# Hybrid decoder layer on one core: v's raw buffers in rising order, two more U steps in the selection, longer runs of V and U products, another order at both ends

## The chip, the cores and the metric

The kernel runs on one core of one Trainium2 chip. The metric is the device time of one launch in microseconds (us). TensorE (PE) does the matrix products, ScalarE (ACT), VectorE (DVE) and GpSimd (POOL) the elementwise work, SyncE (SP) issues most DMAs.

## What is computed

One layer over 512 tokens of width 1024: two token mixers on one input projection, an output projection, then a feed-forward layer that picks for every token and each of 8 heads 16 of 16384 single-neuron experts, and a final norm:

```python
n = rmsnorm(h); proj = n @ w_in; h = h + concat(gla(...), ssd(...)) @ w_out
q = (n2 @ w_query);  s = q . sub_keys            # 2 x 128 scores per token and head
top_s, top_i = top_k(s, 16); best_s, best_pos = top_k(sums of both halves, 16)
gate = softmax(best_s)
out[t] = sum_e gelu(n2[t] . u[e]) * gate[t, e] * v[e]    # e: the chosen experts
y = rmsnorm_final(h + out)
```

## The kernel before

Everything is written in the order in which each engine runs it; there is no scheduler. Products run as three float32r products (`mm3`, lines 107 to 110): each operand is split into a high part (ACT copies it to float32r) and a low part (DVE or POOL subtracts it: `split`, line 102), and hi*hi, hi*lo and lo*hi are summed in PSUM.

Three of the four token tiles (384 tokens) are done densely: all 16384 experts are computed, as 128 blocks of 128, and the gate is zero for those not chosen. The fourth tile goes by indirect DMA: POOL gathers the rows of u and v that each token chose, and DVE multiplies them (`gather`, `use`). The dense blocks have two parts. A **U step** of block e is 24 products of 384 columns (`u_part`, 8 parts of three), whose result goes through a gelu into slot e of `ring`, a buffer of 59 slots. A **V step** of block e is 18 products of 512 columns (`vgrp`, 6 groups of three), which multiply the gated slot e into six PSUM banks (3 token tiles by 2 halves).

The stages in their order, and what the change touches in each:

- *Start.* x is normalised and transposed (`nT`); `ahead` (line 158) loads the blocks of `w_in` into `wraw` and splits them. Block 0 is split inside the loop over `dc`, behind the transposes.
- *Mixers and queries.* Input projection, mixers, output projection, then 16 query blocks with U steps between. Not touched.
- *Selection* (after the queries). DVE's `select(t)` turns places into expert numbers with one-hot tiles (`gat`, float16), `spread(t)` transposes numbers and gates on PE, `spread2(t)` copies them out. Between these calls, `u_run(n)` puts n whole U steps into PE's queue; each one's two low splits run on POOL here.
- *Gates.* For 48 units of 8 tokens, DVE makes one-hot tiles A, eq, B (`gprep`), PE multiplies them to the 128x128 gate tables (`gunit`), DVE multiplies slots 0 to n of `ring` by them, ACT copies the rest: what belongs to blocks 59 to 127 goes into `stage` and in six stores (each 64 tokens) to DRAM (`gd`). U steps run between the units, evenly spread up to block 56; their low splits are on DVE here.
- *V and U.* `vs` is the stream of v (128 blocks, 4 raw buffers, split into pairs). For block e: V groups of half 0, V groups of half 1, and between them the 8 U parts of block e+59. `gload` brings the gates of block e+59 from `gd` into the slot that block e leaves. The pool of v's buffers is made where the pool of A, eq, B and `stage` was closed, so they lie in the same memory.
- *End.* The last two V blocks by token tile (`final`), residual, norm and store; token tile 3 (the gathered one) is ready earlier.

SP issues the DMAs strictly in the order written: a DMA that must wait for its buffer or its data holds all behind it. In `Stream.loads` the raw tiles come from one name with `bufs=nraw`. In the built program the four raw tiles of v are handed out at byte 175424, then 187712, 183616, 179520, of each partition; the two `stage` buffers lie at 171328 to 188992 and 188992 to 206656, and the sixth store reads the second.

The lines of the steps: `Stream.loads` 47, `split` 102, `ahead` 158, `u_part` 1050, `u_run` 1063, the calls of the selection 1087 to 1110, `gunit` 1177, `vs.loads` 1234, `gload` 1251, `final` 1257, the V and U loop 1322 to 1378.

Of the kernel before, what the change touches and what calls it, by code (L numbers as in the profile page):

```python
# [7 lines left out]
F32 = mybir.dt.float32  # L8
F32R = mybir.dt.float32r
# [9 lines left out]
D = 1024  # L19
# [16 lines left out]
class Stream:  # L36
# [9 lines left out]

    def loads(s, upto):
        while s.nl <= min(upto, len(s.src) - 1):
            s.raw[s.nl] = s.c.tile([128, 1024], F32, name=s.nm + "r", bufs=s.nraw)
            s.y.load(s.raw[s.nl], s.src[s.nl])  # L50
            s.nl += 1

# [11 lines left out]
class Layer:  # L64
# [22 lines left out]
    def load(self, out, in_):  # L87
        return self.nc.sync.dma_start(out, in_)
# [10 lines left out]
    def stt(self, out, x, s, y, op0, op1, **k):  # L99
        return self.V.scalar_tensor_tensor(out, x, s, y, op0=op0, op1=op1, **k)  # L100
# [31 lines left out]
    def mixers(self):  # L132
# [104 lines left out]
        def scale(t, half, on_act):  # L237
            x, r = xs[t][:, half * 512:half * 512 + 512], vs_[t][:, 2:3]
            if on_act:
                act(x, x, AF.Copy, scale=r)  # L240
            else:
                V.tensor_scalar(x, x, r, None, op0=OP.mult)
# [13 lines left out]
        scale(2, 0, False)  # L256
        power(vs_[3])
        scale(2, 1, False)
        scale(3, 0, True)
        scale(3, 1, False)  # L260
        nTh, nTl = nt(), nt()
# [3 lines left out]
            for dc in range(8):  # L265
                T.transpose(px[dc][:, t * 128:(t + 1) * 128], xs[t][:, dc * 128:(dc + 1) * 128], ident)
        for dc in range(8):
            if dc == 0:
                ahead(0, 3, 0)
            act(nh[dc], px[dc], AF.Copy, scale=wmix[:, dc:dc + 1])  # L270
            stt(nl[dc], px[dc], wmix[:, dc:dc + 1], nh[dc].bitcast(F32), OP.mult, OP.subtract)
            if dc == 4:
                ahead(0, 3, 1)
# [584 lines left out]
    def experts(self):  # L858
# [117 lines left out]
        def select(t):  # L976

            while any(p[0] == t for p in pieces):
                piece()
            ii = kp.tile([128, 2, 8, 16], F32, name="ii", bufs=2)  # L980
            for e in range(2):
                oh = c.tile([128, 8, 16, 16], F16, name="gat", tag="gat", bufs=3)
                tt(oh, bc(CF[0][:, e, t], 2, 16), bc(itj if e else its, 1, 8), OP.is_equal if e else OP.is_ge)
                tt(oh, oh, TIE[t][:, e], OP.mult)
                for n in (8, 4, 2):
                    tt(oh[:, :, 0:n, :], oh[:, :, 0:n, :], oh[:, :, n:2 * n, :], OP.add)
                tt(ii[:, e], oh[:, :, 0, :], oh[:, :, 1, :], OP.add)
            IX[t] = ii
# [24 lines left out]
        def spread(t):  # L1013
            ii, g = IX.pop(t), bs[:, t]
            p = pt()
            T.transpose(p[:, 0:128], flat(ii[:, 0]), ident)
            T.transpose(p[:, 128:256], flat(ii[:, 1]), ident)
            T.transpose(p[:, 256:384], flat(g), ident)
            act(gs[:, 0, t * 128:(t + 1) * 128], p[:, 256:384], AF.Copy, scale=SC)
            SPR[t] = p  # L1020
# [42 lines left out]
        def u_run(n):  # L1063
            for _ in range(n):
                for i in range(8):
                    u_part(i)
# [27 lines left out]
        ties(2)  # L1094
        u_run(1)
        select(1)
        spread(0)
        u_run(1)
        ties(3)
        select(2)  # L1100
        u_run(2)
# [4 lines left out]
        select(3)  # L1106
        u_run(2)
        spread(2)
        u_run(4)
        spread2(2)  # L1110
        idx = c.tile([128, 128], I32, name="idx")
        gt0 = c.tile([128, 128], F32, name="gt0")
# [118 lines left out]
        vp = ctx.enter_context(tc.tile_pool(name="vp", bufs=1, reuse_waits="tile"))  # L1231
        vs = Stream(self, vp, "v", [a["v"][e * 128:(e + 1) * 128, :] for e in range(NE)], 4)
        HT[0] = htile()
        vs.loads(1)
        u_run(1)
        vs.split(1)
        hprep(0)
        u_run(1)
        vs.loads(3)

        g0 = ng[0]
        share = [0]
# [8 lines left out]
        def gload(e):  # L1251
            if e < NE:
                load(ring[:, e % RS, :], gd3[:, e - RS, :])

        gload(RS)

        def final():

            nv = lambda: c.tile([128, 4], F32, name="rs3", bufs=4)
            hf = [slice(0, 512), slice(512, 1024)]  # L1260
            junk = [c.tile([128, D], F32, name="gat", tag="gat", bufs=3), vp.tile([128, D], F32, name="vr", bufs=4)]
            v = [nv() for _ in range(4)]

            def products(t):
                s = slice(t * 128, t * 128 + 128)
                for n in range(2):
                    for e in (NE - 2, NE - 1):
                        self.mm3(pv[t][n], HT[e][0][:, s], HT[e][1][:, s], *vs.parts[2 * e + n], False, e == NE - 1)

            def residual(t, n):  # L1270
                h = hs[t][:, hf[n]]
                stt(h, pv[t][n], 1.0 / SC, h, OP.mult, OP.add)
                square(t, n)

            def square(t, n):
                act(junk[t % 2][:, hf[n]], hs[t][:, hf[n]], AF.Square, accum_out=v[t][:, n:n + 1])

            def weight(t, n, eng):
                eng.tensor_tensor(hs[t][:, hf[n]], hs[t][:, hf[n]], wf[:, hf[n]], op=OP.mult)

            def mean(t):
                V.tensor_scalar(v[t][:, 2:3], v[t][:, 0:1], EPS * D, None, op0=OP.add)
                V.tensor_scalar(v[t][:, 0:1], v[t][:, 1:2], v[t][:, 2:3], 1.0 / D, op0=OP.add, op1=OP.mult)

            def power(t):
                G.tensor_tensor(v[t][:, 3:4], v[t][:, 0:1], self.mhalf, op=OP.pow)

            def scale(t):
                stt(hs[t], hs[t], v[t][:, 3:4], wf, OP.mult, OP.mult)
                load(self.out[t], hs[t])  # L1290

            square(3, 0)
            square(3, 1)
            mean(3)
            power(3)
            for t in range(3):
                products(t)
            residual(0, 0)
            residual(0, 1)
            scale(3)  # L1300
            mean(0)
            power(0)
            residual(1, 0)
            weight(1, 0, G)
            residual(1, 1)
            weight(1, 1, G)
            scale(0)
            mean(1)
            power(1)
            residual(2, 0)  # L1310
            weight(2, 0, G)
            residual(2, 1)
            weight(2, 1, V)
            act(hs[1], hs[1], AF.Copy, scale=v[1][:, 3:4])
            load(self.out[1], hs[1])
            mean(2)
            power(2)
            act(hs[2][:, hf[0]], hs[2][:, hf[0]], AF.Copy, scale=v[2][:, 3:4])
            V.tensor_scalar(hs[2][:, hf[1]], hs[2][:, hf[1]], v[2][:, 3:4], None, op0=OP.mult)
            load(self.out[2], hs[2])  # L1320

        for e in range(NE):
            todo = [gather] * (plan[e + 1] - plan[e])
            pos = [(2 * i + 1) * 7 // max(1, 2 * len(todo)) for i in range(len(todo))]

            def fill(i, todo=todo, pos=pos):
                while pos and pos[0] <= i:
                    pos.pop(0)
                    todo.pop(0)()

            vs.loads(e + 4)
            if e == NE - 2:

                hprep(e + 1)
                vs.split(2 * e + 2)
                vs.pair = us.pair
                vs.split(2 * e + 3)
                final()
                break
            hh, hl = HT.pop(e)  # L1340

            def vgrp(n, t):
                s = slice(t * 128, t * 128 + 128)
                vh, vl = vs.parts[2 * e + n]
                self.mm3(pv[t][n], hh[:, s], hl[:, s], vh, vl, e == 0, e == NE - 1)

            for i in range(3):
                vgrp(0, i)
                if i == 2:
                    vs.parts.pop(2 * e)  # L1350
                    vs.split(2 * e + 2)
                    hprep(e + 1)
                    gload(e + 1 + RS)
                u_part(i)
                fill(i)
            u_part(3)
            for i in range(3):
                vgrp(1, i)
                if i == 2:
                    vs.parts.pop(2 * e + 1)  # L1360
                    vs.split(2 * e + 3)
                u_part(4 + i)
                fill(3 + i)
            u_part(7)
            fill(6)
            if e == NE - 12:
                for t in (0, 1):
                    hs[t] = us.c.tile([128, D], F32, name="ur", bufs=2)
                    load(hs[t], self.hd[t])
            if e == NE - 4:  # L1370
                while ng[0] < 256 or pend:
                    gather()
                vs.loads(NE - 1)
                wf = c.tile([128, D], F32, name="gat", tag="gat", bufs=3)
                load(wf, a["w_norm_final"].to_broadcast([128, D]))
                hs[2] = c.tile([128, D], F32, name="gat", tag="gat", bufs=3)
                load(hs[2], self.hd[2])
                hs[3] = acc[0]
# [90 lines left out]
```

## Time and profile before

| | us |
|---|---|
| median of 3 runs (lowest, highest) | 1508.53 (1506.76, 1512.19) |
| the profiled execution | 1503.02 |
| its span, first to last instruction | 1501.2 |
| PE busy in it | 1456.2 (97%) |
| DVE busy | 1169.4 (78%) |
| ACT busy | 632.7 (42%) |
| POOL busy | 451.7 (30%) |
| mean granted TensorE clock | 0.991 of 2.4 GHz |

The profile is of one execution, 1.8 us longer outside its span. Matmuls are pipelined and their ends are modelled, so the distance between starts tells the pace of PE. In rows of time the columns are start, duration (us), engine, line, operation and tiles; in brackets the idle time of the engine before it, and what ended it. SPq and ACTq are the queues' own rows: the time at which a DMA is issued, not its transfer.

### The profile page before, as it was taken

Reading aid. Unit: us, or ns where it says so; the run is one execution under the profiler, and the core shown is the slowest. Engines: PE = TensorE matmul, PEld = TensorE weight load, DVE = VectorE, ACT = ScalarE, POOL = GpSimd, SP = SyncE. Lnnn points to the kernel's source line nnn. Section 1 sums busy time; section 2 is a strip of 40 time slices with the busy share of each in tenths; the row PEclk is TensorE's granted clock in tenths of the full one; section 3 lists DMA queues with packets and bytes.
Section 4 is the critical chain, followed back from the end, with each engine's and each line's share of the span. In section 5 each row is a group of like instructions: output and inputs, shape, how many; then the busy total and the mean of one; then the engine's idle time right before and its main releaser. Section 6 shows DMA issues by size and latency. Waiting matters only on the chain.

```text
span 1501.2 us, 22402 instructions
## 1 busy us (share of the span) xinstructions
PE 1456.2 (97%) x7904; PEld 1278.0 (85%) x7904; DVE 1169.4 (78%) x2473; ACT 632.7 (42%) x1201; POOL 451.7 (30%) x380
## 2 busy tenths in 40 slices
PE   7999999999898999979999999999999999999997
PEld 5787778888898999878999999999999998888886
DVE  6542663789999999967877778777788888888886
ACT  5435633433654544433333333333333333444444
POOL 2002404444672000002333333333333333333332
PEclk9999999999999999999999999999999999999999
DMA  5231224222334556658888888889899888888894
GB/s 189 84 126 58 71 73 155 96 85 85 105 104 143 159 167 175 180 181 300 322 316 316 323 312 307 317 305 332 304 331 322 314 316 276 292 300 299 297 325 178
DMA packets 148738, 335.56 MB, mean 224 GB/s; under 512 B 64640, under 2 KB 73872, under 8 KB 148496
## 3 DMA queue, kind: packets, MB, share of 16 engines
q1 hardware_dynamic: 58672, 186.32, 36.1%
q0 software_dynamic: 36864, 134.23, 25.1%
q10 hardware_dynamic: 53088, 13.57, 3.9%
q8 instruction: 62, 1.02, 0.3%
q14 instruction: 52, 0.43, 0.1%
HBM read 315.79 MB, written 18.28 MB: 223 GB/s over the span
## 4 chain that ended last, share of the span: by engine, by line
PE 80%; DVE 12%; issue 3%; DMA 2%; ACT 2%; POOL 0%; SPq 0%; DVEq 0%; POOLq 0%; ACTq 0%
PE pm L109 25%; PE pm L108 25%; PE pm L110 25%; DVE gat L97 4%; PE pg L1186 2%; DVE B L97 1%; DVE ul L104 1%; PE pm L904 1%; DMA gd<-stage 1%; DVE ring L97 1%; DMA ur<-in_uT 1%; DVE eq L97 1%; DVE A L97 1%; ACT b L91 0%; ACT tp L91 0%
## 5 line engine op out<-in xcount | busy, mean ns | idle before, releaser
L108 PE MATMUL pm<-nT,uh 128*128 128x384 f32 (+1 forms) x1152 | 402.1, 349 | 8.8 <-ACT uh L91 8.3
L110 PE MATMUL pm<-nT,ul 128*128 128x384 f32 (+1 forms) x1152 | 397.0, 345 | 2.0 <-POOL ul L104 2.0
L109 PE MATMUL pm<-nT,uh 128*128 128x384 f32 (+1 forms) x1152 | 397.0, 345 | 0.5 <-DVE nT L97 0.5
L109 PE MATMUL pm<-vl,hh 128*128 128x512 f32 x765 | 300.4, 393 | 0.2 <-DVE vl L104 0.2
L110 PE MATMUL pm<-vh,hl 128*128 128x512 f32 x765 | 300.3, 393 | 0.0
L108 PE MATMUL pm<-vh,hh 128*128 128x512 f32 x765 | 299.0, 391 | 0.2 <-ACT vh L91 0.2
L1135 POOL DMA_INDIRECT gat<-in_u,idx x128 | 136.8, 1069 | 473.3 <-DVE gat L100 467.0
L91 ACT ACTIVATE uh<-ur 128x512 fp32r<-128x512 f32 x288 | 180.2, 629 | 214.1 <-PE pm L109 182.0
L108 PEld LDWEIGHTS pm<-nT,uh 128*128 128x128 f32 x1152 | 218.1, 189 | 33.5 <-ACT uh L91 8.7
L109 PEld LDWEIGHTS pm<-nT,uh 128*128 128x128 f32 x1152 | 218.1, 189 | 25.0 <-DVE nT L97 1.1
L110 PEld LDWEIGHTS pm<-nT,ul 128*128 128x128 f32 x1152 | 217.7, 189 | 9.1 <-POOL ul L104 2.9
L1135 POOL DMA_INDIRECT gat<-in_v,idx x128 | 147.2, 1150 | 253.1 <-DVE n2a L100 220.4
L91 ACT ACTIVATE vh<-vr 128x512 fp32r<-128x512 f32 x255 | 159.4, 626 | 136.8 <-PE pm L110 135.4
L104 DVE TENSOR_TENSOR vl<-vr,vh 128x512 fp32r<-128x512 f32 x255 | 175.3, 688 | 37.4 <-ACT vh L91 36.4
L104 DVE TENSOR_TENSOR ul<-ur,uh 128x512 fp32r<-128x512 f32 x206 | 140.7, 689 | 56.8 <-ACT uh L91 56.4
L100 DVE SCALAR_TENSOR_TENSOR n2a<-gat,dots,n2a 128x1024 f32<-128x1024 f32 x128 | 164.0, 1281 | 21.5 <-DMA gat<-in_v,idx 18.5
L110 PEld LDWEIGHTS pm<-vh,hl 128*128 128x128 f32 x765 | 143.7, 188 | 30.9
L100 DVE SCALAR_TENSOR_TENSOR gat<-gat,n2a 128x1024 f32<-128x1024 f32 x128 | 156.2, 1220 | 9.8 <-DMA gat<-in_u,idx 9.6
L108 PEld LDWEIGHTS pm<-vh,hh 128*128 128x128 f32 x765 | 144.0, 188 | 14.2 <-ACT vh L91 0.7
L109 PEld LDWEIGHTS pm<-vl,hh 128*128 128x128 f32 x765 | 144.0, 188 | 14.1 <-DVE vl L104 0.5
L104 POOL TENSOR_TENSOR ul<-ur,uh 128x512 fp32r<-128x512 f32 x82 | 118.7, 1455 | 99.8 <-ACT uh L91 99.4
L91 ACT ACTIVATE gl<-pm 128x384 f32<-128x384 f32 (+16 forms) x104 | 46.0, 442 | 219.8 <-PE pm L110 219.8
(254 smaller groups left out, 1685.2 us busy)
## 6 DMA issues: line engine op xcount, KB each, us to landing
ur<-in_uT SPq DMA_DIRECT2D x128, 512.0 KB, 6.0
vr<-in_v SPq DMA_DIRECT2D x128, 512.0 KB, 5.0
gd<-stage ACTq DMA_DIRECT2D x6, 2208.0 KB, 14.5
ring<-gd SPq DMA_DIRECT2D x69, 192.0 KB, 5.2
wraw<-in_w_in SPq DMA_DIRECT2D x23, 512.0 KB, 4.4
ur<-in_w_query SPq DMA_DIRECT2D x16, 512.0 KB, 3.7
b<-in_x SPq DMA_DIRECT2D x8, 512.0 KB, 3.6
wraw<-in_w_out SPq DMA_DIRECT2D x8, 512.0 KB, 3.9
```

The source lines that it names most:

```text
L91: return self.S.activation(out, in_, f, **k)
L97: return self.V.tensor_tensor(out, x, y, op=op)
L100: return self.V.scalar_tensor_tensor(out, x, s, y, op0=op0, op1=op1, **k)
L104: (self.G if pool else self.V).tensor_tensor(lo, src, hi.bitcast(F32), op=OP.subtract)
L108: T.matmul(out, lhi, rhi, start=start, stop=False)
L109: T.matmul(out, lhi, rlo, start=False, stop=False)
L110: T.matmul(out, llo, rhi, start=False, stop=stop)
L904: T.matmul(p[:, t * 128:(t + 1) * 128], q[:, t * 128:(t + 1) * 128], skT[:, b, :], start=True, stop=True)
L1135: G.indirect_dma_start(out=r, out_offset=None, in_=src, in_offset=bass.IndirectOffsetOnAxis(ap=idx[:, k:k + 1], axis=0))
L1186: T.matmul(o, A[:, t // 2, :, t % 2], B[:, i, t // 2, :, t % 2], start=i == 0, stop=i == 1)
```

## The change

- `Stream.loads`: each raw buffer has its own name, so the tiles lie and are used in rising order (v: 175424, 179520, 183616, 187712).
- Start: block 0 of `w_in` is split in two halves before x's last scaling, ACT then POOL, instead of in the loop behind the transposes.
- Selection: two U steps before `spread(0)` in place of one behind it, and five in place of four before the last `spread2`. Two steps more in all, so the gates stage holds two fewer.
- V: three v blocks are loaded at first in place of two and then two more; the first `gload` moves to the end of block 0's U step, and block 60's with it.
- V and U: three V groups in turn, four U parts, three V groups, four U parts, in place of single groups and parts alternating.
- End: other engines and halves for the last scalings, the last tile stored in two halves, one of them from ACT's queue.

```diff
-            s.raw[s.nl] = s.c.tile([128, 1024], F32, name=s.nm + "r", bufs=s.nraw)
+            s.raw[s.nl] = s.c.tile([128, 1024], F32, name=f"{s.nm}r{s.nl % s.nraw}", bufs=1)
@@ start, before scale(3, ...)
+        parts[0] = b4(F32R), b4(F32R)
+        for k in range(2):
+            f = slice(k * 512, k * 512 + 512)
+            act(parts[0][0][:, f], raws[0][:, f], AF.Copy)
+        for k in range(2):
+            f = slice(k * 512, k * 512 + 512)
+            self.G.tensor_tensor(parts[0][1][:, f], raws[0][:, f], parts[0][0][:, f].bitcast(F32), op=OP.subtract)
+        raws.pop(0)
+        seen[1] = 1
@@
-            if dc == 0:
+            if dc == 1:
                 ahead(0, 3, 0)
@@ selection
         select(1)
+        u_run(2)
         spread(0)
-        u_run(1)
         ties(3)
...
         spread(2)
-        u_run(4)
+        u_run(5)
         spread2(2)
@@ before the V loop
-        vs.loads(1)
+        vs.loads(2)
         u_run(1)
         vs.split(1)
         hprep(0)
         u_run(1)
-        vs.loads(3)
...
-        gload(RS)
-
@@ final
-            weight(1, 1, G)
-            scale(0)
+            residual(2, 0)
+            scale(0, hf[1])
+            load(self.out[0], hs[0])
+            residual(2, 1)
             mean(1)
             power(1)
-            residual(2, 0)
-            weight(2, 0, G)
-            residual(2, 1)
-            weight(2, 1, V)
-            act(hs[1], hs[1], AF.Copy, scale=v[1][:, 3:4])
-            load(self.out[1], hs[1])
+            scale(1, hf[1])
             mean(2)
             power(2)
+            act(hs[1][:, hf[0]], hs[1][:, hf[0]], AF.Copy, scale=v[1][:, 3:4])
+            load(self.out[1], hs[1])
+            weight(2, 0, V)
             act(hs[2][:, hf[0]], hs[2][:, hf[0]], AF.Copy, scale=v[2][:, 3:4])
-            V.tensor_scalar(hs[2][:, hf[1]], hs[2][:, hf[1]], v[2][:, 3:4], None, op0=OP.mult)
-            load(self.out[2], hs[2])
+            self.S.dma_start(self.out[2][:, hf[0]], hs[2][:, hf[0]])
+            scale(2, hf[1])
+            load(self.out[2][:, hf[1]], hs[2][:, hf[1]])
@@ V and U
-            vs.loads(e + 4)
+            vs.loads(e + 4 if e else 2)
...
-                    gload(e + 1 + RS)
+                    if e:
+                        gload(e + 1 + RS)
+                fill(i)
+            for i in range(4):
                 u_part(i)
-                fill(i)
-            u_part(3)
             for i in range(3):
                 vgrp(1, i)
                 if i == 2:
                     vs.parts.pop(2 * e + 1)
                     vs.split(2 * e + 3)
-                u_part(4 + i)
                 fill(3 + i)
+            for i in range(4, 7):
+                u_part(i)
+            if e == 0:
+                gload(RS)
+                gload(RS + 1)
             u_part(7)
```

SP's queue where the V stage begins (`vr` is a raw buffer of v, `ur` one of u, `ring<-gd` a `gload`; the `ur` loads are those of blocks 59 and on). Before:

```order
L88 DMA vr<-in_v 128x1024 x2
L88 DMA ur<-in_uT 128x1024 x2
L88 DMA vr<-in_v 128x1024 x2
L88 DMA ring<-gd 128x384
L88 DMA vr<-in_v 128x1024
```

And now:

```order
L88 DMA vr_6957<-in_v 128x1024
L88 DMA vr_6959<-in_v 128x1024
L88 DMA vr_6961<-in_v 128x1024
L88 DMA ur_6964<-in_uT 128x1024
L88 DMA ur_7010<-in_uT 128x1024
L88 DMA ur_7078<-in_uT 128x1024
L88 DMA ring<-gd 128x384 x2
L88 DMA vr_7133<-in_v 128x1024
```

Three loads of v and three of u now stand ahead of the first `gload`; before it were four of v and two of u, and the second v buffer was the one at byte 187712, half in the second `stage` buffer.

PE's queue in the V and U stage, from the first V group of a block. Before, and the same place now:

```order
L108 MATMUL pm<-vh,hh 128x512
L109 MATMUL pm<-vl,hh 128x512
L110 MATMUL pm<-vh,hl 128x512
L108 MATMUL pm<-nT,uh 128x384
L109 MATMUL pm<-nT,uh 128x384
L110 MATMUL pm<-nT,ul 128x384
```

```order
L108 MATMUL pm<-vh,hh 128x512
L109 MATMUL pm<-vl,hh 128x512
L110 MATMUL pm<-vh,hl 128x512
L108 MATMUL pm<-vh,hh 128x512
L109 MATMUL pm<-vl,hh 128x512
L110 MATMUL pm<-vh,hl 128x512
L108 MATMUL pm<-vh,hh 128x512
L109 MATMUL pm<-vl,hh 128x512
L110 MATMUL pm<-vh,hl 128x512
L108 MATMUL pm<-nT,uh 128x384
```

Nine V products stand in a row, and twelve U products follow; the number of products is the same.

## Rows read from the trace of the kernel before

**Rows 1.** Page, part 1: busy us of each engine

```profile
PE 1456.2 (97%) x7904; PEld 1278.0 (85%) x7904; DVE 1169.4 (78%) x2473; ACT 632.7 (42%) x1201; POOL 451.7 (30%) x380
```

**Rows 2.** Windows: stretch, PE, PEld, DVE, ACT, POOL busy, PEclk, DMA share, GB/s

```profile
380.00:462.00 82.00, 71.95 (x402) 69.90 (x401) 79.66 (x131) 45.26 (x71) 55.51 (x34) 0.98 0.34 116
...
690.00:1440.00 750.00, 750.00 (x3668) 664.39 (x3667) 602.48 (x904) 286.48 (x544) 263.73 (x238) 1.00 0.88 310
```

**Rows 3.** Timeline where the V stage begins, of several engines and queues

```profile
656.49 0.52 ACTq L1199 DMA_DIRECT2D gd<-stage  x1
...
657.78 0.69 DVE L104 TENSOR_TENSOR ul<-ur,uh 128x512 fp32r<-128x512 f32 x1 [0.66 <-ACT uh L91]
...
666.01 0.34 PE L108 MATMUL pm<-nT,uh 128*128 128x384 f32 x1
...
666.53 0.39 PE L108 MATMUL pm<-vh,hh 128*128 128x512 f32 x1
...
669.88 0.33 SPq L88 DMA_DIRECT2D vr<-in_v  x1
...
675.65 0.69 PE L108 MATMUL pm<-nT,uh 128*128 128x384 f32 x1 [8.26 <-ACT uh L91]
...
685.22 0.39 PE L108 MATMUL pm<-vh,hh 128*128 128x512 f32 x1
...
693.54 0.39 PE L108 MATMUL pm<-vh,hh 128*128 128x512 f32 x1
```

**Rows 4.** Page, part 6: DMA issues, count, KB each, median us to landing

```profile
ur<-in_uT SPq DMA_DIRECT2D x128, 512.0 KB, 6.0
...
gd<-stage ACTq DMA_DIRECT2D x6, 2208.0 KB, 14.5
```

**Rows 5.** Waits of PE, 390 to 463 us: total, times, longest

```profile
PE pm L1017 <- DVE ii L97: 3.9, 2, 2.6
PE pg L1186 <- DVE B L97: 3.3, 1, 3.3
...
PE pm L1018 <- DVE bs L97: 1.4, 1, 1.4
```

**Rows 6.** Selection: POOL's splits (397 to 459.7 us, by form), two DVE rows of time

```profile
L104 POOL TENSOR_TENSOR ul<-ur,uh 128x512 fp32r<-128x512 f32 x26 | 44.4, 1722 | 18.7 <-ACT uh L91 18.2 <-PE pm L110 0.2
...
419.48 1.21 DVE L97 TENSOR_TENSOR gat<-tops,itj 128x2048 f16<-128x2048 f16 x1
...
424.68 2.32 DVE L97 TENSOR_TENSOR gat<-tops,its 128x2048 f16<-128x2048 f16 x1
```

**Rows 7.** Gates stage: its window (columns as in Rows 2), and DVE's splits (page, part 5)

```profile
488.00:655.60 167.60, 162.73 (x1354) 153.45 (x1352) 163.67 (x293) 80.99 (x197) 1.15 (x1) 1.00 0.57 164
...
L104 DVE TENSOR_TENSOR ul<-ur,uh 128x512 fp32r<-128x512 f32 x206 | 140.7, 689 | 56.8 <-ACT uh L91 56.4
```

**Rows 8.** The second V product, 690 to 1235 us, then 1245 to 1470 us (by form)

```profile
L109 PE MATMUL pm<-vl,hh 128*128 128x512 f32 x394 | 155.6, 395 | 0.0
...
L109 PE MATMUL pm<-vl,hh 128*128 128x512 f32 x326 | 126.8, 389 | 0.0
```

**Rows 9.** Timeline of the start

```profile
13.67 2.37 POOL L104 TENSOR_TENSOR b<-wraw,b 128x1024 fp32r<-128x1024 f32 x1 [1.78 <-DMA d_skip<-in_d_skip]
...
16.09 0.50 PE L110 MATMUL pm<-nT,b 128*128 128x512 f32 x1 [0.35 <-POOL b L104]
```

**Rows 10.** Timeline of the end

```profile
1492.47 1.28 DVE L100 SCALAR_TENSOR_TENSOR gat<-pm,gat 128x512 f32<-128x512 f32 x2
...
1495.39 0.21 DVE L1283 TENSOR_SCALAR rs<-rs 128x1 f32<-128x1 f32 x1
...
1495.01 1.40 POOL L1279 TENSOR_TENSOR gat<-gat 128x512 f32<-128x512 f32 x1
1496.38 0.54 POOL L1286 TENSOR_TENSOR rs<-rs,mhalf 128x1 f32<-128x1 f32 x1
...
1497.70 0.33 SPq L88 DMA_DIRECT2D out_dram<-gat  x1
```

More of the change, by code (lines that the diff above doesn't have):

```diff
@@ L1260, in final @@
             hf = [slice(0, 512), slice(512, 1024)]
-            junk = [c.tile([128, D], F32, name="gat", tag="gat", bufs=3), vp.tile([128, D], F32, name="vr", bufs=4)]
+            junk = [c.tile([128, D], F32, name="gat", tag="gat", bufs=3), vp.tile([128, D], F32, name=f"vr{NE % 4}", bufs=1)]
             v = [nv() for _ in range(4)]
@@ L1286, in power, with scale @@
                 G.tensor_tensor(v[t][:, 3:4], v[t][:, 0:1], self.mhalf, op=OP.pow)
-            def scale(t):
-                stt(hs[t], hs[t], v[t][:, 3:4], wf, OP.mult, OP.mult)
-                load(self.out[t], hs[t])
+            def scale(t, cols=slice(0, D)):
+                stt(hs[t][:, cols], hs[t][:, cols], v[t][:, 3:4], wf[:, cols], OP.mult, OP.mult)
             square(3, 0)
@@ L1300, in final @@
             scale(3)
+            load(self.out[3], hs[3])
             mean(0)
@@ L1304, in final @@
             weight(1, 0, G)
+            scale(0, hf[0])
             residual(1, 1)
-            weight(1, 1, G)
-            scale(0)
+            residual(2, 0)
+            scale(0, hf[1])
+            load(self.out[0], hs[0])
+            residual(2, 1)
             mean(1)
             power(1)
-            residual(2, 0)
-            weight(2, 0, G)
-            residual(2, 1)
-            weight(2, 1, V)
-            act(hs[1], hs[1], AF.Copy, scale=v[1][:, 3:4])
-            load(self.out[1], hs[1])
+            scale(1, hf[1])
             mean(2)
             power(2)
+            act(hs[1][:, hf[0]], hs[1][:, hf[0]], AF.Copy, scale=v[1][:, 3:4])
+            load(self.out[1], hs[1])
+            weight(2, 0, V)
             act(hs[2][:, hf[0]], hs[2][:, hf[0]], AF.Copy, scale=v[2][:, 3:4])
-            V.tensor_scalar(hs[2][:, hf[1]], hs[2][:, hf[1]], v[2][:, 3:4], None, op0=OP.mult)
-            load(self.out[2], hs[2])
+            self.S.dma_start(self.out[2][:, hf[0]], hs[2][:, hf[0]])
+            scale(2, hf[1])
+            load(self.out[2][:, hf[1]], hs[2][:, hf[1]])
         for e in range(NE):
@@ L1367, in experts @@
                 for t in (0, 1):
-                    hs[t] = us.c.tile([128, D], F32, name="ur", bufs=2)
+                    hs[t] = us.c.tile([128, D], F32, name=f"ur{t}", bufs=1)
                     load(hs[t], self.hd[t])
```

## The prediction

> **What bounds the kernel now.** Read part 1 of the page first: PE is busy 97% of the span [rows 1]. So a change can only win where PE stands idle or where its products come faster. The windows by stage then say where each is possible. In the long V and U stage PE is busy 750.00 of 750 us, while DVE, ACT and POOL all have slack [rows 2]: there only the pace of the products counts. In the selection PE is busy 71.95 of 82 us and DVE 79.66 [rows 2]: DVE sets the end, and PE waits 3.9 and 1.4 us for the transposes of `spread` and 3.3 us for the first B [rows 5]. In the gates stage both are nearly full, PE 162.73 and DVE 163.67 of 167.6 us [rows 7]. The largest single hole is where the V stage begins: PE stands 8.26 us until block 59's U load has landed and been split [rows 3].
>
> **That hole, step by step.** SP issued the second load of v only at 669.88 [rows 3]. It had to wait because its buffer lies half in the second `stage` buffer, which the sixth store, issued at 656.49 [rows 3], was still reading: 13.4 us, near the 14.5 us that these stores take [rows 4]. Block 59's U load stood behind it in SP's queue. PE began its first V group at 666.53, ended it, and could go on only at 675.65. Block 1 began at 685.22, block 2 at 693.54 [rows 3]. A block takes 8.32 us, so block 0 took 18.69, and 10.4 us were lost: the 8.26 of waiting, and some 2 us in products that ran slower right behind it. After the change the first three buffers of v lie below byte 187712, none in the buffer still being stored, and the U loads stand ahead of the first `gload`, which does need the store. Block 59's load can then go as soon as its raw buffer is split, at 657.78 + 0.69 = 658.5 [rows 3]. It shares the DMA engines with the store; even at 7 us, over the 6.0 us of such loads [rows 4], it lands at 665.5, and after 1.3 us of splitting it is there at 667. PE wants it behind three V groups; the six of a block take 8.32 - 4.16 = 4.16 us (the 4.16 of the U step is worked out below), so three take 2.1, and the time is 668.6. So I take **-10.2**. The lower end is -5: half returns if the store, with two v loads and two U loads beside it, pushes everything behind.
>
> **The two U steps in the selection.** Three U products start in 0.52 us (666.01 to 666.53 [rows 3]), so a step of 24 is 4.16 us. Two more are 8.3 us of PE, and go into the 8.6 us that PE waits there now [rows 5]. But DVE sets the end of the selection, and each step brings POOL two low splits more. While POOL splits, DVE's one-hot products last longer: 1.21 us for one of 2048 elements with no split beside it, 2.32 us for its like when a split started with it [rows 6]; 26 splits run in these 63 us, each 1.72 us on average [rows 6]. I take about 1.0 us of DVE for each of four more splits: **+4.0** on the end of the selection. The Trainium skill, SBUF — State Buffer, section "Who interferes with whom", says that a Vector instruction with two SBUF inputs and a GpSimd instruction that reads SBUF exclude one another, and that the loser waits for the whole instruction. The trace agrees that they collide; taken whole, each split would cost its 1.72 us, four of them +6.9, and the sum below would be 2.9 us worse. The lower end is 0, if the splits fall beside DVE's short pieces.
>
> **The gates stage** gets two steps fewer. If PE bounds it, it gets 8.3 us shorter; if DVE does, by four splits of 0.689 us [rows 7], 2.8 us. As both are within 1 us of one another over 167.6 us [rows 7], I take the middle, **-5.5**.
>
> **Longer runs in V and U.** In the stage where U groups follow V groups, the second V product takes 395 ns, in the stage of V alone 389 [rows 8]. I read this as 6 ns on each of the second and third products of a V group that a U group follows. In a block, four of the six groups are now followed by V. Over 69 blocks: 69 x 4 x 2 x 6 ns = **-3.3**. The lower end is 0. The U loads now stand behind the `gload` in SP's queue, the V splits and the gathers come at other places; with PE full and the others not, I cost these at nothing. What covers them is that U's halves are split one block ahead, some 8 us.
>
> **The start.** PE's third product waits until 16.09, as POOL's low split of block 0 ran from 13.67 to 16.04 [rows 9]. The split now stands before ACT's last scaling of x, in time in which ACT waits for POOL. By my estimate POOL is done about 1.7 us earlier, and PE's second chunk, 0.35 us of whose delay is this wait and the rest ACT's copies behind the split, can come 1.0 us earlier. But block 1's split still stands between ACT's copies, so I keep **-0.7**. Ends: -1.2, and +0.3 if `w_in`'s first block lands late and holds ACT's scaling.
>
> **The end.** The last residual is done at 1492.47 + 1.28 = 1493.75, and its norm's sum at 1495.39 + 0.21 = 1495.60; yet POOL's power starts at 1496.38, behind POOL's own 1.40 us of weighting from 1495.01, and the store goes at 1497.70 [rows 10]. The weighting is DVE's now and comes behind the sum, where it lies beside the power; DVE's scaling of half of tile 1 comes before the sum in its place. So the power starts 0.8 us earlier, and the halves on two queues give a little more: **-0.9**, ends 0 and -1.8.
>
> **The sum.** -10.2 + 4.0 - 5.5 - 3.3 - 0.7 - 0.9 = -16.6. Against the profiled execution that is 1503.02 - 16.6 = 1486.4. The median of the runs, 1508.53, is 5.5 us above that execution; against it the same sum gives **1491.9**. With all the good ends it would be 1483, with all the bad ones 1508.
>
> **The rivals.**
>
> 1. *The hole moves.* The first `gload` still waits for the sixth store and now holds the loads of v blocks 3 to 5 and of block 62 behind it; DVE must have block 59's gates before it splits for block 2. For it: the store and five loads share the engines. Against: PE has block 1 whole in its buffers, 8.3 us from about 675. If half of the 10.2 returns, 1491.9 + 5.1 = 1497.0.
> 2. *DVE stays the bound through selection and gates.* Every split holds DVE for its whole 1.72 us [rows 6]: +6.9 in place of +4.0, and the gates stage shrinks by 2.8 in place of 5.5. That is 5.6 us worse, 1497.5. For it: DVE is busy 163.67 of 167.6. Against: PE's share there is as high. The lock that the Trainium skill states in the section named above is what this rival takes at its full length.
> 3. *The runs change nothing.* The 6 ns belong to the stage (its DMA, its other engines) and not to the change between V and U; then this part doesn't do what it is to do: 1495.2. For it: the two windows differ in more than the order. Against: U's own pace is the same in the stage of gates, where nothing of V runs.
> 4. *Slower: U's loads come late in every block.* SP must now issue the `gload` first, and that waits for the slot's split on DVE, so a U load goes behind the three V groups and two splits, by my estimate some 3.6 us later in each block. ACT asks for its data some 6 us after that, and the median landing is 6.0 us [rows 4]. What PE still has is about 7 us, the block by which splits run ahead. Should landings pass 13 us, PE would wait in each of 69 blocks; from 16.6 / 69 = 0.24 us a block on, the kernel is slower than before; at 0.35 us it takes 1491.9 + 24.2 = 1516. Against: the DMA share is 0.88 and the bytes are the same [rows 2].
>
> **How the numbers follow.** Forecast 0.54, rivals in order 0.13, 0.15, 0.15, 0.03. Forecast and the first three rivals all lie more than 4.5 us (0.3%, about what a measurement of this kernel can tell from no change) below 1508.53; several of them together could come within it. So faster 0.92, same 0.05, slower 0.03. The range takes in the single rivals up to 1497.5 and some of two together, and the good ends of gates and start: 1484.5 to 1500.5.
>
> **What would show it.** In the changed profile PE's wait for the ACT split at the beginning of the V stage is gone or under 1 us, and U's loads are issued near 658 to 662. PE's wait for `ii` is moved to the third `spread`, and the first gate unit comes 3 to 5 us later with POOL at 30 splits. The gates stage is 3 to 8 us shorter. The second V product averages about 391 ns between the start of the V stage and the last U step. I am wrong if the hole is still there or PE has new waits in the V and U stage, or if gates and selection together are longer than before.

## The result, and the profile after

The changed kernel's median is 1492.27 us (four runs, 1491.13 to 1493.41) against 1507.87 (four runs): a ratio of 0.9891, 95% interval 0.987 to 0.9913. Its profiled execution took 1492.95 us, span 1491.2. Against the profiled execution of before that is 10.07 us less, while the medians are 15.6 apart; where the other 5.5 us are is the main question below.

Page part 1 of the changed kernel, answering to [rows 1]; then three windows of it (columns as in [rows 2], [rows 7]):

```profile
PE 1458.2 (98%) x7904; PEld 1279.5 (86%) x7904; DVE 1163.3 (78%) x2469; ACT 637.0 (43%) x1200; POOL 467.7 (31%) x383
```

```profile
380.00:465.00 85.00, 80.28 (x454) 77.22 (x453) 82.76 (x145) 48.66 (x78) 59.43 (x37) 1.00 0.37 118
690.00:1230.00 540.00, 540.00 (x2720) 490.19 (x2719) 425.01 (x683) 207.35 (x391) 195.19 (x171) 1.00 0.89 318
500.00:654.00 154.00, 147.04 (x1220) 136.83 (x1220) 151.29 (x270) 71.52 (x176) 1.14 (x1) 1.00 0.57 162
```

In the selection PE now stands idle 4.7 us of 85 where it stood 10.05 of 82; DVE is as full as before.

Timeline where the V stage begins, changed kernel, answering to [rows 3] (SP's rows are its queue):

```profile
651.07 1.33 SPq L88 DMA_DIRECT2D vr<-in_v  x3
655.01 0.52 ACTq L1208 DMA_DIRECT2D gd<-stage  x1
657.02 9.00 SPq L88 DMA_DIRECT2D ur<-in_uT  x3
672.61 0.80 SPq L88 DMA_DIRECT2D ring<-gd  x2
...
665.04 0.39 PE L108 MATMUL pm<-vh,hh 128*128 128x512 f32 x1
667.10 0.34 PE L108 MATMUL pm<-nT,uh 128*128 128x384 f32 x1
673.38 0.39 PE L108 MATMUL pm<-vh,hh 128*128 128x512 f32 x1
681.72 0.39 PE L108 MATMUL pm<-vh,hh 128*128 128x512 f32 x1
```

Three loads of v go out before the store and three of u behind it, the last of them by 666.02; none waits for the store to land, as the first two `gload` do, which come last. PE goes from V to U at 667.10 with no wait, and block 0 takes 8.34 us instead of 18.69.

PE's waits from 390 to 468 us, answering to [rows 5]:

```profile
PE pm L110 <- POOL ul L104: 3.1, 4, 1.2
PE pm L1026 <- DVE ii L97: 1.3, 1, 1.3
PE pg L1195 <- DVE B L97: 1.1, 1, 1.1
```

What PE waits for most there is now POOL's low split.

The lengths of the stages, from the starts of PE's products in eight traces (us; e1 to e12 are the experiments; "mixers" runs from the second mixer's first product to the last score, "selection" from there to the first gate product, "gates" to the last one, "V and U" over 68 blocks from block 1 to block 69, "V alone" from there to the first product of the last V group, "tail" from the end of PE's last product):

| | before | after | e1 | e2 | e3 | e5 | e9 | e12 |
|---|---|---|---|---|---|---|---|---|
| first projection product to first `wg` product | 12.00 | 11.49 | 12.01 | 12.01 | 11.51 | 12.02 | 12.00 | 11.49 |
| mixers to last score | 201.1 | 204.1 | 202.2 | 202.3 | 201.3 | 201.0 | 201.0 | 199.7 |
| selection | 89.77 | 92.69 | 89.24 | 92.70 | 93.01 | 89.57 | 88.96 | 92.91 |
| gates | 192.89 | 186.52 | 193.79 | 186.55 | 188.04 | 192.59 | 192.52 | 186.82 |
| V block 0 | 18.69 | 8.34 | 8.32 | 19.00 | 8.32 | 18.70 | 18.85 | 8.32 |
| V and U | 565.76 | 567.12 | 568.89 | 565.76 | 569.28 | 574.92 | 567.12 | 565.76 |
| V alone | 241.12 | 241.13 | 241.15 | 241.12 | 241.14 | 241.15 | 241.31 | 241.11 |
| tail | 8.29 | 8.68 | 8.28 | 8.30 | 8.68 | 8.29 | 8.28 | 7.86 |

### The profile page after: what moved, and what is told of

Its sections match the earlier page's. It is cut to its first block, busy times and chain, and to the rows that moved or that the text cites. A ratio compares the mean times of both kernels' runs of the same rounds, so it can differ in the third digit from the quotient of the medians.

```text
span 1491.2 us, 22545 instructions
## 1 busy us (share of the span) xinstructions
PE 1458.2 (98%) x7904; PEld 1279.5 (86%) x7904; DVE 1163.3 (78%) x2469; ACT 637.0 (43%) x1200; POOL 467.7 (31%) x383
## 4 chain that ended last, share of the span: by engine, by line
PE 81%; DVE 13%; issue 3%; ACT 2%; DMA 1%; POOL 0%; POOLq 0%; DVEq 0%; SPq 0%; ACTq 0%
PE pm L108 25%; PE pm L109 25%; PE pm L110 25%; DVE gat L97 4%; PE pg L1195 2%; DVE B L97 1%; DVE ul L104 1%; DVE eq L97 1%; DVE ring L97 1%; PE pm L913 1%; DVE A L97 1%; ACT b L91 0%; ACT tp L91 0%; DMA ur<-in_uT 0%; PE pm L275 0%
## 5 line engine op out<-in xcount | busy, mean ns | idle before, releaser
L1144 POOL DMA_INDIRECT gat<-in_u,idx x128 | 146.2, 1142 | 444.0 <-DVE gat L100 439.0
L1144 POOL DMA_INDIRECT gat<-in_v,idx x128 | 150.6, 1176 | 252.2 <-DVE n2a L100 227.3
L104 POOL TENSOR_TENSOR ul<-ur,uh 128x512 fp32r<-128x512 f32 x86 | 124.5, 1456 | 99.8 <-ACT uh L91 95.9
L104 DVE TENSOR_TENSOR ul<-ur,uh 128x512 fp32r<-128x512 f32 x202 | 137.4, 685 | 18.2 <-ACT uh L91 17.9
L91 ACT ACTIVATE gl<-pm 128x384 f32<-128x384 f32 (+15 forms) x102 | 45.4, 445 | 235.1 <-PE pm L110 235.1
```

The lines of the kernel that those rows point to most:

```text
L91: return self.S.activation(out, in_, f, **k)
L104: (self.G if pool else self.V).tensor_tensor(lo, src, hi.bitcast(F32), op=OP.subtract)
L1144: G.indirect_dma_start(out=r, out_offset=None, in_=src, in_offset=bass.IndirectOffsetOnAxis(ap=idx[:, k:k + 1], axis=0))
```

## The experiments

**The hole: e1 and e7.** e1 is the kernel before with the transition alone; e7 has only its first line, the names.

```diff
-            s.raw[s.nl] = s.c.tile([128, 1024], F32, name=s.nm + "r", bufs=s.nraw)
+            s.raw[s.nl] = s.c.tile([128, 1024], F32, name=f"{s.nm}r{s.nl % s.nraw}", bufs=1)
@@ e1 only
-        vs.loads(1)
+        vs.loads(2)
...
-        vs.loads(3)
...
-        gload(RS)
...
-            vs.loads(e + 4)
+            vs.loads(e + 4 if e else 2)
...
-                    gload(e + 1 + RS)
+                    if e:
+                        gload(e + 1 + RS)
...
+            if e == 0:
+                gload(RS)
+                gload(RS + 1)
             u_part(7)
```

> The kernel before with the transition part alone: rising raw names, three v loads first, the first two gload at the end of block 0, V and U groups still alternating. If SP's queue behind the sixth store was the whole hole, block 0 takes 8.3 to 8.5 us in place of 18.69, no half clock follows, and the time is 10 us (9 to 11.5) below before. If the hole only moves on to the gload, PE waits 3 to 6 us in block 1 to 3 and the time is 4 to 7 us below.

> The kernel before with the rising raw names alone; the first gload still stands before the loop and four v loads are still issued ahead of it. If the place of the second v buffer was the whole cause, block 59's U load goes out near 659, block 0 takes 8.3 to 9 us and the time falls by some 10 us. If the moved gload is needed too, SP still stands behind the store with the fourth v buffer or the gload, and block 0 or 1 keeps a wait of 3 to 8 us.

Measured: e1 0.9884 (0.9858 to 0.991) of before, median 1495.83 against 1512.9; e7 0.995 (0.9926 to 0.9973). In e1 block 0 takes 8.32 us, and the half clock behind the hole (0.5 granted, 1.2 GHz, from 669.31 to 679.55 us in the trace of before) is gone. Its time falls by 17 us, more than the 9 to 11.5 expected; e5 and e6 below bear on the rest. In e7 block 0 takes 8.32 too, but blocks 1 and 2 take 9.75 and 11.46. Its timeline, SP's queue and then PE:

```profile
659.17 3.52 SPq L88 DMA_DIRECT2D ur<-in_uT  x2
662.74 11.25 SPq L88 DMA_DIRECT2D vr<-in_v  x2
674.04 0.43 SPq L88 DMA_DIRECT2D ring<-gd  x1
...
685.26 0.50 PE L108 MATMUL pm<-vh,hh 128*128 128x512 f32 x1 [1.26 <-ACT hh L91]
686.80 0.69 PE L109 MATMUL pm<-vl,hh 128*128 128x512 f32 x1 [1.04 <-DVE vl L104]
```

The names let block 59's U load through, but now the fourth v buffer lies in the one being stored, SP stands until 674, and the work behind it comes late two blocks on. The names alone are not enough: they give rival 1, the hole that moves. The moved loads alone were not run.

**The selection: e2.** Before, with two U steps ahead of `spread(0)` and five ahead of the last `spread2`.

```diff
+        u_run(2)
         spread(0)
-        u_run(1)
...
-        u_run(4)
+        u_run(5)
```

> The kernel before with the two more U steps in the selection alone. By the prediction the selection gets 4.0 us longer and the gates stage 5.5 us shorter: -1.5 us. By what the pair of traces shows (+2.9 and -6.4): -3.5. If DVE pays each split in full (rival 2): +4.1. The hole at the V stage stays, 18 to 20 us for block 0.

Measured: 0.9979 (0.9951 to 1.0007), so the runs' times alone do not tell it from no change; by stages selection +2.93, gates -6.34, together -3.4, as in the changed kernel. That is 0.73 us of DVE for each of POOL's four splits more, not 1.72: rival 2 is out. The Trainium skill (SBUF — State Buffer, "Who interferes with whom") calls the port pair that the two engines share an exclusive lock; held for four whole splits it would be +6.9, and that is not what these four cost on the end of the selection.

**The order of V and U: e3, e4, e9.** e3 is the changed kernel alternating again, e4 has 18 V and then 24 U, e9 is the kernel before with nine and twelve alone.

```diff
@@ e3
+                u_part(i)
                 fill(i)
-            for i in range(4):
-                u_part(i)
+            u_part(3)
...
+                u_part(4 + i)
                 fill(3 + i)
-            for i in range(4, 7):
-                u_part(i)
@@ e4, in place of the two loops over groups and parts
+            for n in range(2):
+                for i in range(3):
+                    vgrp(n, i)
...
+                    fill(3 * n + i)
+            for i in range(7):
+                u_part(i)
```

> The changed kernel with the V and U groups alternating again as before. If longer runs are worth the 6 ns on two products of each group, block pitch goes from 8.34 to 8.39 and the time up by 3.3 us. If the order is what lost 20 ns a block in the trace of the changed kernel, the pitch is 8.32 again and V and U together 1.4 us shorter. If the 20 ns came from the loads or gathers and not from the order, the pitch stays at 8.34.

> The changed kernel with 18 V products in turn and then 24 U products. U alone starts a product every 173.3 ns, V alone every 226.7: a block without any loss would be 8.24 us, alternating is 8.32, nine and twelve is 8.34. If each change between V and U costs a fixed 13 ns (six a block in the kernel before: 80 ns), the pitch is 8.25 to 8.27 and the time 5 to 6 us below the changed kernel. If the loss belongs to the V products wherever U stands in the same block, the pitch stays at 8.32 to 8.35 and the time is the same to 1 us.

> The kernel before with nine V and twelve U products in turn and nothing else; the hole stays. Alternating leaves the hole at 8.32 us a block in one trace and 8.44 in two. If the longer runs have one pace whatever PE waited for, blocks behind the hole are 8.34, V and U take 567 us against 574 to 575 in the two traces of before near its median, and the median falls by 6 to 8 us. If they have a slower pace behind a wait too, blocks are 8.40 to 8.50 and the median stays within 3 us. By the prediction's own term: -3.3.

Measured: e3 1492.69, e4 1494.38, e9 1504.78 (0.9981 of before, 0.9964 to 0.9999; its median 5.0 below that of before in the same comparison, 1509.8, its ratio 2.9). None came out quite as expected: e3 keeps its 8.32 us only to block 48, e4 is slower than both of its readings, and e9 has the blocks of its first one, but its median falls by less than 6. Blocks take 8.34 us in the changed kernel from the first to the last, 8.37 in e4, 8.34 in e9 although the hole stands before them. In e3 they take 8.32 up to block 48, and from block 50 on 8.44. What lies between is in e3's timeline, SP's queue, DVE and PE:

```profile
1064.29 0.33 SPq L88 DMA_DIRECT2D n2a<-hd  x1
...
1071.02 1.28 DVE L100 SCALAR_TENSOR_TENSOR n2a<-gat,dots,n2a 128x1024 f32<-128x1024 f32 x1 [4.79 <-DMA n2a<-hd]
...
1072.95 0.49 PE L109 MATMUL pm<-vl,hh 128*128 128x512 f32 x1 [0.62 <-DVE vl L104]
```

Where the gathered rows change from u to v, DVE waits 4.79 us for the load of h into the sum, `vl` of the next block stands behind it, PE waits 0.62 us, and block 49 takes 9.57, and each of the 19 behind it 0.12 us more than those ahead. In e1 a wait of PE of 0.23 us at the same place did the same. In the changed kernel DVE waits there too, but 2.58 us, and PE not at all.

**Before once more: e5 and e6.** No edit.

> The kernel before unchanged, for another trace of it: its executions spread from 1502 to 1515.5 us, those without the hole only from 1489 to 1497, at like clocks. If the pace at which PE comes out of the hole differs between executions, one of over 1510 us shows blocks of 8.42 to 8.46 us where the trace at hand shows 8.32 (69 x 0.12 = 8.3 us). If the hole itself or the stages ahead of it vary, the blocks are 8.32 again and the difference stands in those stages.

> The same kernel once more, for a second chance at an execution of over 1510 us; the same two readings: blocks of 8.42 to 8.46 us behind the hole, or blocks of 8.32 and another stage longer.

Measured: 1511.98 and 1512.64 us; in both, blocks behind the hole take 8.44 us to the end, but for block 49 of e5, which takes 9.44 with a wait of 0.5 us for `vl`. e5's timeline, then its window of 300 us, and the same window of before (8.32) and of the changed kernel (8.34):

```profile
675.53 0.69 PE L108 MATMUL pm<-nT,uh 128*128 128x384 f32 x1 [8.41 <-ACT uh L91]
...
684.96 0.39 PE L108 MATMUL pm<-vh,hh 128*128 128x512 f32 x1
...
693.40 0.39 PE L108 MATMUL pm<-vh,hh 128*128 128x512 f32 x1
```

```profile
700.00:1000.00 300.00, 300.00 (x1495) 270.43 (x1494) 233.78 (x399) 110.41 (x214) 99.25 (x93) 1.00 0.89 312
```

```profile
700.00:1000.00 300.00, 300.00 (x1516) 271.56 (x1515) 237.36 (x406) 111.75 (x216) 100.29 (x94) 1.00 0.88 314
```

```profile
700.00:1000.00 300.00, 300.00 (x1512) 272.45 (x1511) 235.50 (x410) 114.05 (x217) 109.55 (x97) 1.00 0.89 318
```

PE is busy all 300 us in each, at clock 1.00, and starts 1495, 1516 and 1512 products. V and U take 574.92 us in e5 and 573.92 in e6, against 565.76 in the trace at hand: that trace was of one of the shorter executions. Nine of 17 executions of before in the last comparison took over 1509 us, eight 1501 to 1508.7.

Where the 0.12 us are, by PE's groups from 700 to 1000 us, mean ns of one: before, e5, changed kernel.

```profile
L109 PE MATMUL pm<-nT,uh 128*128 128x384 f32 x289 | 97.3, 337 | 0.0
...
L108 PE MATMUL pm<-nT,uh 128*128 128x384 f32 x288 | 96.6, 335 | 0.0
L109 PE MATMUL pm<-vl,hh 128*128 128x512 f32 x217 | 85.7, 395 | 0.0
...
L108 PE MATMUL pm<-vh,hh 128*128 128x512 f32 x217 | 84.8, 391 | 0.0
```

```profile
L109 PE MATMUL pm<-nT,uh 128*128 128x384 f32 x285 | 96.9, 340 | 0.0
L108 PE MATMUL pm<-nT,uh 128*128 128x384 f32 x284 | 96.3, 339 | 0.0
...
L109 PE MATMUL pm<-vl,hh 128*128 128x512 f32 x214 | 85.0, 397 | 0.0
L108 PE MATMUL pm<-vh,hh 128*128 128x512 f32 x214 | 84.5, 395 | 0.0
```

```profile
L109 PE MATMUL pm<-nT,uh 128*128 128x384 f32 x288 | 97.3, 338 | 0.0
L108 PE MATMUL pm<-nT,uh 128*128 128x384 f32 x288 | 97.3, 338 | 0.0
...
L109 PE MATMUL pm<-vl,hh 128*128 128x512 f32 x216 | 84.9, 393 | 0.0
L108 PE MATMUL pm<-vh,hh 128*128 128x512 f32 x216 | 84.1, 389 | 0.0
```

Every kind of product is some ns longer in e5. In the changed kernel V's are shorter and U's longer than before. These durations hold modelled ends; for the changed kernel the distances between starts, given with the longer runs below, tell the same.

**Mending what lost: e8, e10, e11, e12.** e8 and e12 are the changed kernel alternating, e11 keeps nine and twelve; all three begin the sum of gathered v rows without a load (h is added later), put `mean(2)` ahead of tile 1's scaling at the end and store the last tile at once. e10 is the changed kernel as it is.

```diff
@@ gather: h is loaded at j == 192 and added at 256
...
-                    load(acc[0], self.hd[GT])
+            elif j == 128:
+                V.tensor_scalar(acc[0], r, gw[:, 0:1], None, op0=OP.mult)
+            elif j == 256:
+                tt(acc[0], acc[0], r, OP.add)
@@ final
             power(1)
-            scale(1, hf[1])
+            weight(2, 0, V)
             mean(2)
             power(2)
+            scale(1, hf[1])
...
-            weight(2, 0, V)
...
-            self.S.dma_start(self.out[2][:, hf[0]], hs[2][:, hf[0]])
             scale(2, hf[1])
-            load(self.out[2][:, hf[1]], hs[2][:, hf[1]])
+            load(self.out[2], hs[2])
```

> The changed kernel with V and U alternating, the sum of gathered v rows begun without a load (h is added later), and at the end the mean of tile 2 ahead of the scaling of tile 1, its weighting in DVE's gap before, one store. If blocks are 8.32 us by their order and went to 8.44 in the alternating run only because PE waited once for DVE behind that load, all 69 blocks are 8.32 and V and U take 565.8 (567.1 in the changed kernel, 569.3 in the alternating run). The tail from the last V product's group to the end: 7.4 to 7.8 us if POOL's power was slowed by DVE's weighting beside it (0.92 us in place of 0.54) and the two halves stored cost the rest, 8.7 if not. In all 2.3 to 2.7 us below the changed kernel, by stages.

> The changed kernel unchanged, for a comparison on one chip with the two runs that follow: blocks of 8.34 us from block 0 on, V and U 567.1, tail 8.7.

> The changed kernel, nine and twelve kept, with the sum of gathered v rows begun without a load and the mended end. Blocks of 8.34, V and U 567.1; the tail 7.9 in place of 8.7. If the stages ahead fall alike, 0.8 us below the changed kernel.

> The alternating order with the mended sum and end once more, beside the changed kernel: V and U 565.8 against 567.1 and the tail 7.9 against 8.7, 2.1 us below the changed kernel by stages. If a wait of PE anywhere in V and U comes in some executions, blocks behind it go at 8.44, V and U take up to 574, and the median is not below that of the changed kernel.

Measured: e8 1492.45; on one chip e10 1490.15 (1489.68 to 1490.95), e11 1490.96 (1489.45 to 1492.14), e12 1490.35 (1486.63 to 1493.87). In e8 and e12 all blocks take 8.32 us and V and U 565.76, as expected; in e10 and e11 8.34. The tail is 7.9 us in e8, e11 and e12, 8.65 in e10. Yet the medians agree: the stages' 2 us are less than the executions of e12 differ, and e11, expected 0.8 us below e10, is 0.8 above it. e12's six lie nearly in the order of their granted clocks, from 1486.63 at 0.999 to 1493.87 at 0.993. Its traced execution is the shortest of all and has no half clock between 10.5 and 1481 us; those of e8, e10 and e11 each have one to four stretches of 3.4 to 6.8 us at 0.5 ahead of the V stage, and some 1.4 us go with each 3.4 (the mixers take 199.7 us in e12 and 201.0 in e10, which has one). In e11 PE also waited 0.47 us where V stands alone (242.15 us there), for a `vl` ahead of which DVE had waited 2.28 us for a gathered row. No version is shown to beat the changed kernel.

## Why the prediction was right, and where not

The sign and the largest term came as forecast. That the time came within 0.4 us is luck: two errors cancel, 6.5 us in the sum and 6.2 in what was carried from the trace to the median. The steps in the pair of traces:

| step | predicted | measured |
|---|---|---|
| hole | -10.2 | -10.35 |
| selection | +4.0 | +2.92 |
| gates | -5.5 | -6.37 |
| V and U | -3.3 | +1.36 |
| start, to the first `wg` product | -0.7 | -1.24 |
| end | -0.9 | +0.39 |
| mixers to last score, not foreseen | 0 | +3.06 |
| all the rest | 0 | +0.16 |
| sum | -16.6 | -10.07 |

- **The hole** was right in cause and size; e1 shows it alone, e7 that the names by themselves do not close it. Rival 1 is out for the change, and is what the names alone would do.
- **Selection and gates**: right in sign, and e2 repeats them to 0.1 us. By the pair a split costs DVE 0.73 us and not 1.0; but the old selection takes 88.9 to 89.8 us in six traces and the new one 92.7 to 93.1 in eight, so 0.7 to 1.1 is what they can tell. The gates gain more than -5.5 by a term that the prediction did not have, the clock. Their first 25 us, before and in the changed kernel:

```profile
463.00:488.00 25.00, 24.51 (x193) 23.60 (x193) 21.77 (x42) 11.61 (x27) 1.36 (x2) 0.93 0.38 126
467.00:492.00 25.00, 24.12 (x211) 23.05 (x211) 24.16 (x45) 12.34 (x28) 3.71 (x3) 1.00 0.46 149
```

  Before, the clock was granted at 0.5 from 464.51 to 467.92 us, behind PE's 3.3 us wait for B [rows 5]; in the changed kernel that wait is 1.1 us, and the clock stays at 1.00. e3 and e8, which have the two steps more and 3.4 us at 0.5, take 188.0 us in the gates; the six other traces with the two steps, which have none, take 186.5 to 186.8. So the steps are worth some -4.9 and the clock -1.5. Whether the shorter wait is what keeps the clock up is not shown: e3 and e8 wait 1.3 us there.
- **Longer runs** failed as a term. "I read this as 6 ns on each of the second and third products of a V group that a U group follows" leaves out what U does, which I put at nothing. By the distances between PE's starts (means of blocks 5 to 44), the 18 V products of a block take 4.165 us before and 4.145 now, 20 ns less where I counted 48; the 24 U products take 4.155 before and 4.195 now, 40 ns more, twice the gain. Both fall in one half of the block (V from 2.082 to 2.063, the U behind it from 2.078 to 2.116); the other half is as before. In e4, with 18 and 24, V takes 4.131 and U 4.236. So longer runs do shorten V, but U loses more. V's second product averages 393 ns and not the 391 named as a sign. In an execution at 8.32 us the change of order costs 0.02 us a block, +1.36. Rival 3, that runs change nothing, comes near where the hole is gone: in one comparison e12 (alternating) has 1490.35 and e11 1490.96. It misses what runs do behind a wait: alternating, PE goes at 8.32 or 8.44 us a block, and was at 8.44 behind a wait in e1, e3, e5, e6 and e7; nine and twelve went at 8.34 behind the same hole in the one trace of e9. Against e5 and e6 the runs are worth 6.8 to 7.8 us.
- **From the profiled execution to the median** was the second error. I carried the 5.5 us between them over to the changed kernel as if it had them too. It has not: its trace is within 0.7 us of its median. The slower pace that e5 and e6 show behind the hole, 8.2 to 9.2 us more in V and U than in the trace at hand, is enough for those 5.5 us, and the change leaves no wait there to start it. That this pace is what lifts the median is argued from times, as the executions behind the median were not traced. In the last comparison before's executions lie up to 10 us apart at one granted clock (1501.14 and 1511.54 at 0.993), while e9's rise evenly as the clock falls, from 1503.41 to 1504.88 at 0.992 to 1509.73 and 1510.61 at 0.987. That e1 alone gives 17 us by medians, where the hole is 10.35, and e9 alone 5.0, fits this.
- **The start**: 0.51 us between the first product and `wg` come back in every trace with the new start; the other 0.73 is when the first product begins, which varies from 14.15 to 15.07 with the old start too.
- **The end** failed. The rows of the changed kernel, answering to [rows 10]:

```profile
1484.32 0.75 DVE L100 SCALAR_TENSOR_TENSOR ur<-ur,rs,gat 128x512 f32<-128x512 f32 x1 [0.66 <-POOL rs L1292]
...
1485.24 0.21 DVE L1289 TENSOR_SCALAR rs<-rs 128x1 f32<-128x1 f32 x1
1485.37 0.68 DVE L1285 TENSOR_TENSOR gat<-gat 128x512 f32<-128x512 f32 x1
1485.54 0.92 POOL L1292 TENSOR_TENSOR rs<-rs,mhalf 128x1 f32<-128x1 f32 x1 [1.25 <-DVE rs L1289]
...
1487.24 0.39 ACTq L1326 DMA_DIRECT2D out_dram<-gat  x1
1487.27 0.33 SPq L88 DMA_DIRECT2D out_dram<-gat  x1
```

  The power does start earlier, 3.91 us behind the first product of the last V group (1481.63) where it was 4.29, but by 0.4 us and not 0.8: the sum ends 3.82 us behind that product, before 3.51, as DVE's 0.75 us of scaling tile 1 stands ahead of it. And DVE's weighting, which I laid "beside the power", starts 0.17 us ahead of the power and makes it 0.92 us instead of 0.54; the store goes 5.64 us behind that product, before 5.61. Here the Trainium skill's section named above (SBUF — State Buffer, "Who interferes with whom") does apply, in kind: it says that a DVE instruction with two SBUF inputs contends with a GpSimd instruction that reads SBUF. Here POOL's power was held some 0.4 us, and DVE's weighting, 0.68 us, was not. In e12 the weighting stands ahead of tile 1's power instead, and that one takes 0.93 us and tile 2's 0.55; the store goes 1.07 us earlier behind PE's last product, and the tail is 0.8 us shorter. The last half lands 3.91 us after its issue, the whole tile before 3.54: that is the +0.39. The halves are not shown to be the reason, for e12's whole tile takes 4.16.
- **The mixers' +3.06** goes with the clock: in the changed kernel's trace it was granted at 0.5 from 182.53 to 189.36 and from 213.25 to 216.66 us, in that of before for 3.41 us from 198.27. e10, the same program as the changed kernel, has 3.41 us at 0.5 there and takes 201.0.
- Rival 4 did not come: from block 1 to block 69 PE waits nowhere in the traces of the changed kernel and of e10.

## What to carry to other kernels

Look at the order in which buffers are handed out where one pool takes another's memory: a load whose buffer was still being stored stopped everything behind it in SP's queue, and here the names alone only moved the hole two blocks on. A wait can cost more than its length, for the work behind it may go on at another pace: compare the pitch of a loop before and behind each wait, and in more than one execution. Before an offset between a trace and the median is carried over, find out which stage holds it.

## What was not expected of the hardware

With PE full, at clock 1.00 and no wait recorded, the same 42 products took 8.320 or 8.440 us, to 1 ns the same for 19 to 69 blocks on end, and the pace changed only where PE had waited (in e5 the wait at block 49 did not change it). Nine and twelve gave 8.340 in four traces, 18 and 24 8.367. Alone, V products start every 226.7 ns and U products every 173.3, which would make 8.24. So mixing costs 0.08 or 0.20 us a block in alternation, 0.10 in runs of nine and twelve, 0.13 in 18 and 24. What in PE holds the pace was not found. The Trainium skill, TensorE: Matmul & The Clock Gate, section "Back-to-back issue gap", says that in a stream of weight loads and products the spacing is set by both, pipelined through a window of pending instructions; no run here shows whether that is the cause. Nor is it settled why the hole left before at 8.32 in two traces (that at hand and e2) and at 8.44 in two.
